# Decode steps around the attentions of a hybrid decoder: a pause, two closer paces, and key pages in quarters

## The chip, the cores and the metric

One Trainium2 chip, one of its cores. The metric is the device time of one execution of the whole program, in microseconds (us); of several runs the median is given. The engines are called by the names of the profile: PE (TensorE matmul) with its weight loads PEld, DVE (VectorE), ACT (ScalarE), POOL (GpSimd), SP (SyncE, which only issues DMAs here).

## What is computed

One inference step of a decoder layer for two groups that share the weights: a prompt of 1024 rows, and 8 sample rows that each look back on 8192 cached positions.

```
# prompt (1024 rows) and, with the same weights, samples (8 rows)
q, k, v, logf, u, z = mixer_inputs(rmsnorm(x), w_in)      # z: gelu, rmsnorm
x = x + concat(rmsnorm(fox_attend(q, k, v, logf)), rmsnorm(u * gate(z))) @ w_o
mk, mv = rmsnorm(mem) @ w_ck, rmsnorm(mem) @ w_cv         # prompt: 256 memory rows
x = x + cross_attend(rmsnorm(x), mk, mv) @ w_co           # samples: cached mk, mv
x = x + conv_ffn(rmsnorm(x))                              # 1024 -> 2 x 2816 -> 1024
```

The attention has 8 heads of 64 with a forget gate. For the samples its keys and values come from a paged cache (64 pages of 128 positions for each of 8 samples). The large products are done as three float32r matmuls of high and low parts.

## The kernel before, in words

**The prompt's work** is a chain of Python generators, and each `yield` states an estimate of the PE time that its piece takes. `p1` does the input projection: for q, the gates and u, k, v and z in turn, 8 tiles of 128 rows against 512 columns. The last four z tiles are done together (`by_rows(4, ws)`, L569): 8 yields of 2.6, then 4 of 0.1. Just ahead of them `early()` (L568) emits the first head pair's set-up of the first attention (L701 to L744) and the opening of `pmem`, which loads the memory rows and the first four blocks of `w_ck`. Then:

- `att0`: `attention(0)` for the first 512 rows (four head pairs, 8 score blocks each). `mix` sets beside it, yield for yield, a fill: `pmem`'s 8 products of 5.2 (2 weights x 2 column halves x 2 row tiles) and the first half of the gating (8 yields of 1).
- `att1`: `attention(1)` for the other 512 rows, without a fill.
- `mid0`, `ffn0`, `mid1`, `ffn1`: merge (transposes at L888), output projection, cross-attention and feed-forward for each half of the rows.

Weights come through `wload` (L249): SP issues a load of 512 KB into one of 4 `wr` buffers (L247), ACT writes the high part (L233), DVE the low part (L234), PE multiplies (L270 to L272). In the attention a score block (L759 to L763) is followed by its row maximum on DVE (L765, or L768 where it is two banks wide), the exponential on ACT (L766 or L769), transposes (L787) and the product with the values (L803). In `attention(1)` POOL copies half of the keys' high part (L735) and loads the gate rows (L709, L721).

**The samples' attention** is the generator `decode` (L1303 on), one step for each of 148 turns of its loop. A step gathers one K page of 128 x 2048 with an indirect DMA from POOL (L1354), multiplies it by the query on DVE (L1360) and reduces it to scores (L1364). Every second step gathers two V pages (L1413); the step after it multiplies them on PE (L1419). All K and V pages share four `kv` buffers. K's DVE work is queued behind the newest DVE instruction of the prompt (`behind(ENG.DVE)`), V's matmuls behind the newest of PE.

**Pacing.** The last loop of `build` sets the order: each yield `t` of the prompt is added to an account, and a decode step is emitted for every `PACE[phase]` in it, at most `int(t / PACE) + 1` of them for one yield. A step yields 1 itself; a smaller yield `w` puts back (1 - w) x PACE. `phase[0]` is the stage above, and `held` stops the decode in a few places. What runs after the cache is read (`sample_rest`) is paced by `rest`.

```
acc[0] += t
most = int(t / PACE[phase[1] or phase[0]]) + 1
while bgs and not held[0] and most and acc[0] >= PACE[phase[1] or phase[0]]:
```

The emitted order is not yet that of the engines: the framework's planner simulates the program, and each engine takes what is ready by order of emission. So a gather can start ahead of its place once a buffer is free.

`kstep` splits a page in two halves (`KS = 2`) in the attentions and the mid stages, and takes it whole elsewhere.

Of the kernel before, what the change touches and what calls it, by code (L numbers as in the profile page):

```python
# [12 lines left out]
ALU = mybir.AluOpType  # L13
AX = mybir.AxisListType
PSUM = bass.MemoryType.PSUM
ENG = mybir.EngineType
# [56 lines left out]
KS = 2  # L73
BKQ = 1
LA = (2, 2)
PACE = {'p1': 7.0, 'att0': 20.0, 'mid0': 8.0, 'ffn0': 8.5, 'att1': 15.0, 'mid1': 6.8, 'ffn1': 2.5, 'rest': 2.9}


def build(nc, tc, ctx, a, phases=None):
# [186 lines left out]
    def gemm3(out, pairs):  # L266

        n = len(pairs)
        for i, (sh, sl, mh, ml) in enumerate(pairs):
            mmul(out, sh, mh, start=(i == 0), stop=False)  # L270
            mmul(out, sh, ml, start=False, stop=False)  # L271
            mmul(out, sl, mh, start=False, stop=(i == n - 1))  # L272


    xsT = const.tile([P, 8, 32], F32, tag="xsT", name="xsT")
# [57 lines left out]
    def p1(early):  # L333
# [205 lines left out]
        for tt in range(8):  # L539
            if tt < 4:  # L540
                ps = BK()
                mm_chunk(tt, ws, ps, 0, 512)
                if tt == SD - 1:
                    sps = [sample_copy(*sps[0])]
                if tt == SD:
                    sp = sample_sum(*sps[0])
                    zs = T2()[:8]
                    nc.scalar.activation(zs, sp, AF.Gelu_apprx_tanh, scale=rsk)
                    ssv = sm([8, 1], "sss", 1)
                    ssq_into(ssv, zs)  # L550
                    r = rstd_of(ssv, AW, 1, "r1")
                    nc.vector.scalar_tensor_tensor(zs, zs, r, gs8, op0=ALU.mult, op1=ALU.mult)
                    nc.sync.dma_start(a["o_zs"], zs)

                    mxs = T2()[:8].rearrange("p (h d) -> p h d", d=64)
                    nc.vector.tensor_tensor(
                        mxs, zs.rearrange("p (h d) -> p h d", d=64), ws00[:, 0:8].unsqueeze(2).broadcast_to((8, 8, 64)), op=ALU.mult
                    )
                    nc.vector.tensor_tensor(mxs, mxs, ws00[:, 8:16].unsqueeze(2).broadcast_to((8, 8, 64)), op=ALU.add)
                    usv = us.rearrange("p (h d) -> p h d", d=64)  # L560
                    nc.vector.tensor_tensor(usv, usv, mxs, op=ALU.mult)
                    ssv = sm([8, 1], "sss", 1)
                    ssq_into(ssv, us)
                    r = rstd_of(ssv, AW, 1, "r1")
                    nc.vector.tensor_scalar(us, us, r, None, op0=ALU.mult)
                    nc.sync.dma_start(us_d, us)
            else:
                if tt == 4:  # L568
                    early()  # L569
                    pss = yield from by_rows(4, ws)  # L570
                ps = pss[tt - 4]
            z = T2()
            nc.scalar.activation(z, ps, AF.Gelu_apprx_tanh, scale=rstd[:, tt : tt + 1])
            ssq_into(ssz[:, tt : tt + 1], z)
            nc.scalar.dma_start(zg_d[tt * P : (tt + 1) * P, :], z)
            yield 5.2 if tt < 4 else 0.1
# [62 lines left out]
    def pmem():  # L639
        rm = const.tile([P, 2], F32, tag="rm", name="rm")  # L640
        ssm = sm([P, 2], "ssm", 1)
        for mt in range(2):
            t = U([P, D])
            nc.sync.dma_start(t, a["mem"][mt * P : (mt + 1) * P, :])
            ssq_into(ssm[:, mt : mt + 1], t)
        r = rstd_of(ssm, D, 2, "r2")
        nc.vector.tensor_copy(rm, r)
        mh, ml = [], []
        for q in range(2):
            h, l = U([P, 4, 256], F32R), U([P, 4, 256], F32R)  # L650
            raw = WRAW(1024).rearrange("p (k m) -> p k m", m=256)
            nc.sync.dma_start(raw, a["memT"][q * 512 : (q + 1) * 512, :].rearrange("(k p) m -> p k m", p=P))
            for k in range(4):
                kk = q * 4 + k
                split(raw[:, k, :], h[:, k, :], l[:, k, :], scale=gp[:, G_MEM + kk : G_MEM + kk + 1])
            mh.append(h)
            ml.append(l)
        ahead = [wraw(wpair(a["w_ck"], kk, 0, 512), 1024) for kk in range(4)]
        before = newest(ENG.Activation)
        yield 0.1  # L660
        for w, dst in ((a["w_ck"], mk_d), (a["w_cv"], mv_d)):
            for n in range(2):
                with tc.issue_after(before):
                    ws = [wload(wpair(w, kk, n * 512, 512), 1024, ahead.pop(0) if ahead else None) for kk in range(4)]
                for mt in range(2):
                    ps = MM()
                    ms_ = slice(mt * P, (mt + 1) * P)
                    gemm3(
                        ps[:, :512],
                        [  # L670
                            (mh[k // 4][:, k % 4, ms_], ml[k // 4][:, k % 4, ms_], ws[k // 2][0][:, k % 2, :], ws[k // 2][1][:, k % 2, :])
                            for k in range(8)
                        ],
                    )
                    t = T2()
                    nc.scalar.activation(t, ps[:, :512], AF.Copy, scale=rm[:, mt : mt + 1])
                    nc.scalar.dma_start(dst[mt * P : (mt + 1) * P, n * 512 : (n + 1) * 512], t)
                    yield 5.2


# [621 lines left out]
    def decode():  # L1302
# [48 lines left out]
        def kstep(b, ch, st):  # L1351
            qb, s = st
            kv = KV()
            nc.gpsimd.indirect_dma_start(kv, None, a["cache_k"], off(kidx[:, b, ch : ch + 1]))  # L1354
            kvv = kv.rearrange("p (k c) -> p k c", c=512)
            sp = KS if phase[0][:3] in ("att", "mid") or held[0] else 1
            m = 4 // sp
            with behind(ENG.DVE):
                for i in range(0, 4, m):
                    nc.vector.tensor_tensor(  # L1360
                        kvv[:, i : i + m, :], kvv[:, i : i + m, :], qb.unsqueeze(1).broadcast_to((P, m, 512)), op=ALU.mult
                    )
                for i in range(0, 4, m):
                    nc.vector.tensor_reduce(  # L1364
                        s[:, ch * 4 + i : ch * 4 + i + m, :].rearrange("p k h -> p (k h)"),
                        kvv[:, i : i + m, :].rearrange("p k (h d) -> p (k h) d", d=64),
                        axis=AX.X,
                        op=ALU.add,
                    )


        def soft_max(b, st, dt_):
# [31 lines left out]
        def soft_sum(b, lp):  # L1404
            ps = MS()
            with behind(ENG.PE):
                mmul(ps[:8, :1], lp, ones[:, 0:1], start=True, stop=True)
            nc.vector.tensor_copy(lT[:, b : b + 1], ps[:8, :1])
# [45 lines left out]
        for g in range(8 * 16 + 16 + VLAG + 2):  # L1454
            b, ch = divmod(g, 16)
            if ch == VLAG + 1 and 2 <= b < 10:
                vend(b - 2, vm[b - 2])
            if ch == 0 and 1 <= b < 9:
                dg[b - 1] = soft_all(b - 1, pm[b - 1])
            if ch == 1 and 1 <= b < 9:  # L1460
                lp[b - 1] = soft_exp(b - 1, st[b - 1], dg[b - 1])
            if ch == 2 and 1 <= b < 9:
                soft_sum(b - 1, lp[b - 1])
            if b < 8:
                kstep(b, ch, st[b])
                if ch == 11:
                    A[b] = gates_scan(b)
                if ch == 13:
                    dt_[b] = gates(b, A[b])
                if ch == 14 and b < 7:  # L1470
                    st[b + 1] = prep(b + 1)
                if ch == 15:
                    pm[b] = soft_max(b, st[b], dt_[b])
            if pend:

                pend.pop()()
                pend.pop()(newest(ENG.PE))
                if vch == 15:
                    vm[vb] = vmask(vb, dv[vb])
            vb, vch = divmod(g - 16 - VLAG, 16)  # L1480
            if 0 <= vb < 8 and vch % 2:
                if vch == 1:
                    dv[vb] = DV()
                pend += [vstep(vb, c, st[vb], dv[vb]) for c in (vch - 1, vch)]
            yield 1


    def rms8(src):
# [358 lines left out]
    for t in prompt():  # L1847
        ins = nc.cur_bb.bb.instructions
        for e in (ENG.DVE, ENG.PE):
            for i in range(len(ins) - 1, max(seen, len(ins) - 400) - 1, -1):  # L1850
                if ins[i].engine == e:
                    last[e] = ins[i]
                    break
        acc[0] += t
        most = int(t / PACE[phase[1] or phase[0]]) + 1
        while bgs and not held[0] and most and acc[0] >= PACE[phase[1] or phase[0]]:
# [100 lines left out]
```

## Time and profile before

| | us |
|---|---|
| median of 3 timed runs | 1864.72 |
| lowest and highest of them | 1860.55, 1866.24 |
| the profiled execution | 1858.95 |
| its span, first to last instruction | 1857.2 |
| PE busy | 1779.9 |
| DVE busy | 1390.5 |
| ACT busy | 749.2 |
| POOL busy | 488.5 |

All details below are of the profiled execution. A busy PE is not PE at its peak, since matmuls overlap and their ends are modelled; a PE that idles, or runs at a granted clock below 1, is time lost for certain. In rows of waits the engine ahead of the arrow stood idle, and what stands behind it released it. In a timeline the columns are the start, the length, engine, line, operation, output and inputs with their shapes, and the idle time before it in brackets.

### The profile page before, as it was taken

The numbers are of one execution on the slowest core, as the hardware profiler recorded it, in microseconds if no ns is written. First come the engines' busy times: TensorE is split into PE (matmuls) and PEld (weight loads), VectorE is DVE, ScalarE is ACT, GpSimd is POOL, SyncE is SP. The second block draws the span as 40 slices with busy tenths as digits, with TensorE's granted clock in tenths as the row PEclk, the third lists the DMA queues.
The fourth block names the chain that finished last, engine by engine and source line by source line (L and its number), as shares of the span: only waits on it lengthen the run. The fifth ranks groups of instructions, "written<-read, shape, count | busy, mean of one in ns | idle before, by whom it ended". The sixth has DMA issues, their size and how long they took to land.

```text
span 1857.2 us, 24238 instructions
## 1 busy us (share of the span) xinstructions
PE 1779.9 (96%) x9239; PEld 1290.3 (69%) x9239; DVE 1390.5 (75%) x1666; ACT 749.2 (40%) x1365; POOL 488.5 (26%) x437
## 2 busy tenths in 40 slices
PE   8999998878998999999999999999999999999998
PEld 5887666556676757777777777766576668767765
DVE  4788567876688787989989899898975549754344
ACT  6332355565633535332324234235353334232232
POOL 1243342242122222224332232233322111111110
PEclk9999999999999999999999999999999999999999
DMA  8877889684596976768768789988879588577971
GB/s 318 291 268 262 311 302 346 230 255 150 187 400 228 349 258 262 278 249 326 293 246 339 269 312 363 360 308 338 332 275 348 198 298 266 199 270 265 342 277 60
DMA packets 157012, 521.27 MB, mean 281 GB/s; under 512 B 20808, under 2 KB 40520, under 8 KB 124128
## 3 DMA queue, kind: packets, MB, share of 16 engines
q0 software_dynamic: 57168, 341.14, 49.0%
q1 hardware_dynamic: 92816, 165.99, 25.6%
q10 hardware_dynamic: 6912, 12.59, 1.8%
q8 instruction: 73, 1.20, 0.3%
q14 instruction: 43, 0.35, 0.1%
HBM read 495.73 MB, written 23.93 MB: 280 GB/s over the span
## 4 chain that ended last, share of the span: by engine, by line
PE 67%; DVE 10%; issue 9%; DMA 9%; ACT 4%; POOL 2%; SPq 0%; POOLq 0%; DVEq 0%; ACTq 0%
PE ba L270 9%; PE ba L271 9%; PE ba L272 9%; PE dv L1419 5%; PE bb L271 5%; PE bb L270 4%; PE bb L272 4%; DMA kv<-cache_v,kidx 2%; DVE kv L1360 2%; DMA kv<-cache_k,kidx 2%; DVE s L1364 2%; PE ba L1008 1%; DVE wl L234 1%; PE ba L1010 1%; PE ba L1009 1%
## 5 line engine op out<-in xcount | busy, mean ns | idle before, releaser
L233 ACT ACTIVATE wh<-wr 128x1024 fp32r<-128x1024 f32 (+2 forms) x220 | 229.0, 1044 | 493.1 <-PE ba L271 159.3
L234 DVE TENSOR_TENSOR wl<-wr,wh 128x1024 fp32r<-128x1024 f32 (+2 forms) x220 | 262.2, 1200 | 142.2 <-PE ba L272 54.5
L1354 POOL DMA_INDIRECT kv<-cache_k,kidx x128 | 185.3, 1448 | 611.5 <-DVE s L1364 376.6
L1360 DVE TENSOR_TENSOR kv<-kv,d 128x1024 f32<-128x1024 f32 (+1 forms) x185 | 295.6, 1628 | 42.6 <-DMA kv<-cache_k,kidx 42.5
L1364 DVE TENSOR_REDUCE s<-kv 128x16 f32<-128x1024 f32 (+1 forms) x185 | 295.9, 1619 | 0.1
L1413 POOL DMA_INDIRECT kv<-cache_v,kidx x128 | 171.3, 1338 | 294.4 <-PE dv L1419 191.9
L271 PE MATMUL ba<-u,wh 128*128 128x512 f32 (+1 forms) x560 | 220.6, 394 | 2.3 <-DVE u L237 2.1
L270 PE MATMUL ba<-u,wh 128*128 128x512 f32 (+1 forms) x560 | 219.8, 394 | 1.3 <-ACT u L236 1.1
L272 PE MATMUL ba<-u,wl 128*128 128x512 f32 (+1 forms) x560 | 219.7, 393 | 0.0
L270 PE MATMUL ba<-wh,u 128*128 128x512 f32 (+1 forms) x495 | 185.6, 378 | 1.4 <-DVE u L740 1.0
L271 PE MATMUL ba<-wl,u 128*128 128x512 f32 (+1 forms) x495 | 186.3, 377 | 0.0
L272 PE MATMUL ba<-wh,u 128*128 128x512 f32 (+1 forms) x495 | 184.2, 376 | 0.0
L1419 PE MATMUL dv<-kv,s 128*32 128x512 f32 x1024 | 130.5, 618 | 7.0 <-DMA kv<-cache_v,kidx 6.8
L270 PEld LDWEIGHTS ba<-u,wh 128*128 128x128 f32 x560 | 106.0, 190 | 33.8 <-issue 9.3
L271 PEld LDWEIGHTS ba<-u,wh 128*128 128x128 f32 x560 | 106.4, 190 | 33.1 <-issue 7.1
L272 PEld LDWEIGHTS ba<-u,wl 128*128 128x128 f32 x560 | 106.3, 190 | 32.5 <-issue 10.1
L271 PE MATMUL bb<-u,wh 128*128 128x512 f32 (+1 forms) x304 | 118.2, 389 | 1.7 <-DVE u L237 1.7
L270 PE MATMUL bb<-u,wh 128*128 128x512 f32 (+1 forms) x304 | 118.0, 389 | 0.5 <-ACT u L236 0.5
L272 PE MATMUL bb<-u,wl 128*128 128x512 f32 (+1 forms) x304 | 116.8, 384 | 0.0
L270 PEld LDWEIGHTS ba<-wh,u 128*128 128x128 f32 x495 | 92.9, 188 | 26.5 <-issue 5.9
L271 PEld LDWEIGHTS ba<-wl,u 128*128 128x128 f32 x495 | 93.1, 188 | 22.2 <-issue 5.9
L272 PEld LDWEIGHTS ba<-wh,u 128*128 128x128 f32 x495 | 93.1, 188 | 19.9 <-issue 3.1
(437 smaller groups left out, 3197.5 us busy)
## 6 DMA issues: line engine op xcount, KB each, us to landing
wr<-w_up SPq DMA_DIRECT2D x88, 512.0 KB
kv<-w_up POOLq DMA_DIRECT2D x22, 1024.0 KB, 7.0
wr<-w_down SPq DMA_DIRECT2D x40, 512.0 KB
kv<-w_down POOLq DMA_DIRECT2D x11, 1024.0 KB, 8.0
wr<-w_in SPq DMA_DIRECT2D x16, 512.0 KB
wr<-w_o SPq DMA_DIRECT2D x16, 512.0 KB
wr<-w_cq SPq DMA_DIRECT2D x16, 512.0 KB
wr<-w_co SPq DMA_DIRECT2D x16, 512.0 KB
```

What stands on the lines that cost most here:

```text
L233: nc.scalar.activation(h, src, AF.Copy)
L234: nc.vector.tensor_tensor(l, src, h.bitcast(F32), op=ALU.subtract)
L270: mmul(out, sh, mh, start=(i == 0), stop=False)
L271: mmul(out, sh, ml, start=False, stop=False)
L272: mmul(out, sl, mh, start=False, stop=(i == n - 1))
L1008: mmul(pss[i], mh[k][:, tb], wh, start=(k == korder[0]), stop=False)
L1009: mmul(pss[i], mh[k][:, tb], wl, start=False, stop=False)
L1354: nc.gpsimd.indirect_dma_start(kv, None, a["cache_k"], off(kidx[:, b, ch : ch + 1]))
L1360: nc.vector.tensor_tensor(kvv[:, i : i + m, :], kvv[:, i : i + m, :], qb.unsqueeze(1).broadcast_to((P, m, 512)), op=ALU.mult)
L1364: nc.vector.tensor_reduce(s[:, ch * 4 + i : ch * 4 + i + m, :].rearrange("p k h -> p (k h)"), kvv[:, i : i + m, :].rearrange("p k (h d) -> ...
L1413: nc.gpsimd.indirect_dma_start(kv, None, a["cache_v"], off(kidx[:, b, ch : ch + 1]))
L1419: mmul(dv[32 * j : 32 * j + 32, :], s[:, ch * 4 : ch * 4 + 4, :].rearrange("p k h -> p (k h)"), kvv[:, j, :], start=(ch == 1), stop=(ch == ...
```

## The change

Three edits in one, and nothing in what is computed.

- **Pause.** From the place where `early()` is called to the end of the first `pmem` product, yields of the prompt count 0 in the account, so that no decode step is emitted.
- **Paces.** A step for each 16 (before 20) in `att0`, and for each 10 (before 15) in `att1`.
- **Quarters.** In the attentions `kstep` becomes a sequence of four parts with a yield of 0.2 before each: multiply and reduce 512 columns of the page. The step then yields 0.2 more. In the mid stages the two halves stay, elsewhere the whole page.

```
-PACE = {'p1': 7.0, 'att0': 20.0, 'mid0': 8.0, 'ffn0': 8.5, 'att1': 15.0, 'mid1': 6.8, 'ffn1': 2.5, 'rest': 2.9}
+PACE = {'p1': 7.0, 'att0': 16.0, 'mid0': 8.0, 'ffn0': 8.5, 'att1': 10.0, 'mid1': 6.8, 'ffn1': 2.5, 'rest': 2.9}
...
+    paused = [False]
...
                 if tt == 4:
+                    paused[0] = True
                     early()
                     pss = yield from by_rows(4, ws)
...
                     nc.scalar.dma_start(dst[mt * P : (mt + 1) * P, n * 512 : (n + 1) * 512], t)
+                    paused[0] = False
                     yield 5.2
...
-            sp = KS if phase[0][:3] in ("att", "mid") or held[0] else 1
+            if phase[0][:3] == "att":
+
+                for i in range(4):
+                    yield 0.2
+                    with behind(ENG.DVE):
+                        nc.vector.tensor_tensor(kvv[:, i, :], kvv[:, i, :], qb, op=ALU.mult)
+                        nc.vector.tensor_reduce(
+                            s[:, ch * 4 + i, :], kvv[:, i, :].rearrange("p (h d) -> p h d", d=64), axis=AX.X, op=ALU.add
+                        )
+                return 0.2
+            sp = KS if phase[0][:3] == "mid" or held[0] else 1
...
+            return 1
...
+            left = 1
             if b < 8:
-                kstep(b, ch, st[b])
+                left = yield from kstep(b, ch, st[b])
...
-            yield 1
+            yield left
...
+        if paused[0]:
+            t = 0.0
         acc[0] += t
```

## The prediction

> **What bounds the kernel now.** I read the page first (busy shares, the 40 slices), then the busy table by stage, then the waits of PE and ACT in the stages that lose time, then the timelines there.
>
> ```profile
> PE 1779.9 (96%) x9239; PEld 1290.3 (69%) x9239; DVE 1390.5 (75%) x1666; ACT 749.2 (40%) x1365; POOL 488.5 (26%) x437
> PE   8999998878998999999999999999999999999998
> ```
>
> PE is busy for 1779.9 of 1857.2 us, so all that can be gained without removing matmuls is 77 us of idle time and whatever a lowered clock costs. Each digit is the busy share of 46.4 us in tenths: the weak slices are the first, the last, the seventh to tenth (279 to 464 us) and the thirteenth. Next the stages around the weak group.
>
> ```profile
> 224.00:263.00 39.00, 39.00 (x188) 29.03 (x187) 26.30 (x29) 21.21 (x41) 17.02 (x17) 1.00 0.81 284
> 263.00:295.00 32.00, 23.68 (x119) 14.55 (x118) 21.60 (x21) 15.03 (x32) 13.47 (x8) 0.89 1.03 400
> 295.00:340.00 45.00, 43.47 (x240) 32.78 (x239) 37.27 (x50) 29.50 (x60) 14.60 (x22) 1.00 0.82 290
> 263.00:385.00 122.00, 102.01 (x568) 71.53 (x567) 93.57 (x142) 68.77 (x160) 42.83 (x49) 0.94 0.85 308
> 385.00:512.00 127.00, 111.91 (x761) 78.71 (x761) 88.01 (x127) 81.45 (x173) 27.49 (x31) 0.95 0.59 184
> 512.00:560.00 48.00, 48.00 (x229) 36.01 (x228) 40.67 (x46) 18.61 (x32) 11.03 (x9) 1.00 1.02 399
> ```
>
> Columns: window, length, busy us of PE, PEld, DVE, ACT, POOL, granted clock, DMA share, GB/s. The last z tiles end at about 263; the first attention runs to about 385 with the memory's products between its pieces, the second to about 512. PE is full before (39.00 of 39.00) and after (48.00 of 48.00), and loses 20.0 us in the first attention and 15.1 in the second. The worst stretch is 263 to 295: 8.3 us idle and a clock of 0.89, with the DMA engines at a share of 1.03.
>
> ```profile
> 268.00:272.00 4.00, 0.65 (x5) 0.16 (x8) 2.22 (x5) 2.34 (x4) 1.31 (x1) 0.98 1.01 402
> 272.00:276.00 4.00, 4.00 (x20) 1.50 (x13) 0.31 (x1) 1.07 (x3) 1.80 (x2) 0.59 1.05 429
> 288.00:292.00 4.00, 2.51 (x14) 1.14 (x18) 3.42 (x4) 1.33 (x2) 0.00 (x0) 0.61 1.01 383
> ...
> PE dv L1419 <- DMA kv<-cache_v,kidx: 3.4, 1, 3.4
> PE ms L803 <- ACT t L794: 3.3, 2, 2.1
> PE ba L701 <- DMA t<-q_d: 1.0, 1, 1.0
> PE bb L787 <- ACT t L766: 0.7, 1, 0.7
> ...
> ACT wh L233 <- DMA wr<-w_ck: 6.6, 3, 2.9
> ACT wh L233 <- DMA wr<-w_cv: 2.8, 1, 2.8
> ```
>
> These four waits of PE (columns: us, times, longest) add up to 8.4 us, the whole idle time. Two name a DMA. The other two name ACT, and ACT itself had stood before its weight splits for 9.4 us of DMA: in the timeline below the split at 288.11 comes 1.01 us late, the copy L794 runs behind it at 289.07, and PE gets on at 289.49 after 2.06 us.
>
> ```profile
> 288.11 1.06 ACT L233 ACTIVATE wh<-wr 128x1024 fp32r<-128x1024 f32 x1 [1.01 <-DMA wr<-w_ck]
> 289.07 0.36 ACT L794 ACTIVATE t<-bb 128x256 f32<-128x256 f32 x1
> ...
> 289.49 1.54 PE L803 MATMUL ms<-t,u 128*64 128x256 f32 x6 [2.06 <-ACT t L794]
> ...
> 260.67 8.23 SPq L247 DMA_DIRECT2D wr<-w_ck  x4
> ...
> 263.14 2.88 POOL L1354 DMA_INDIRECT kv<-cache_k,kidx  x1 [0.19 <-issue]
> ...
> 282.20 1.73 POOL L1354 DMA_INDIRECT kv<-cache_k,kidx  x1 [2.67 <-DVE s L1364]
> ```
>
> Four weight loads of 512 KB are issued from 260.67 on; the last was split only at 288.11. From 263.14 to 282.20 five gathers of 1 MB each start (128 x 2048 x 4 bytes; the first and the last are shown), some 12.5 us of the DMA engines' time at the 402 to 429 GB/s of the rows. **So decode gathers starve the memory's weights here.** That stall is what the pause addresses.
>
> **The change, part by part.** First, how many decode steps move. I add up the yields. Behind the point where the pause begins stand 8 x 2.6 + 4 x 0.1 = 21.2 in p1; at a pace of 7 that is 3 steps, and the remainder carried into it makes it 4. The first attention yields 74.6, the fill (memory products, gating) 49.6: 124.2 / 20 = 6 steps. The second yields 74.6 / 15 = 5. Together 15. Afterwards: 0, then 124.2 / 16 = 7 and a part, then 74.6 / 10 = 7 and a part: again 15. From the first merge on, both kernels stand at the same step and have the same paces. So everything is decided between 245 and 512 us; what is gained there reaches the end, since PE is the bound behind it.
>
> *The pause.* A V pair and two K pages are gathered and then held through the pause, because their users are emitted behind it, and with four kv buffers no gather can start until the first is used. The next K step comes 16 units after the last count, some 14 us of yields after the first product: at about 280 on this clock. The five gathers above then do not stand beside the w_ck loads. The stretch 263 to 295 should look like 295 to 340, where the same products run with a loss of 1.53 in 45 us: 1.1 in 32. Idle time goes from 8.3 to 1.1: **-7.2 us**. The lowered clock cost (1 - 0.59) x 4.00 + (1 - 0.61) x 2.51 = 2.6 us beside it; I take **-2.5**. What is late next: on resuming, up to three gathers (3 MB, 7 us at 429 GB/s) start together near 285, when the w_cv loads are due. Bounds of this part: 0 (the stall only moves) and -11.
>
> ```profile
> 380.00:384.00 4.00, 2.45 (x11) 2.06 (x12) 3.34 (x6) 2.57 (x10) 2.35 (x4) 0.63 0.99 339
> 384.00:388.00 4.00, 4.00 (x17) 2.61 (x15) 2.35 (x8) 2.61 (x10) 0.00 (x0) 0.51 1.06 308
> ...
> 381.55 0.48 PE L787 MATMUL bb<-cp,t 128*128 128x128 f32 x1 [2.67 <-ACT t L766]
> ```
>
> The clock term rests on gaps of 3.35 us at most; here 2.67 us of idleness is followed by 0.63 and 0.51. [...]
>
> *Quarters.* Cost first.
>
> ```profile
> L1364 DVE TENSOR_REDUCE s<-kv 128x16 f32<-128x1024 f32 x22 | 26.3, 1207 | 0.1
> L1360 DVE TENSOR_TENSOR kv<-kv,d 128x1024 f32<-128x1024 f32 x22 | 25.8, 1215 | 0.0
> L1364 DVE TENSOR_REDUCE s<-kv 128x32 f32<-128x2048 f32 x3 | 6.8, 2279 | 0.0
> L1360 DVE TENSOR_TENSOR kv<-kv,d 128x2048 f32<-128x2048 f32 x2 | 4.6, 2288 | 4.2 <-DMA kv<-cache_k,kidx 4.2
> ```
>
> These are the K steps from 263 to 512: 63.5 us, 13 pages. Halving 2048 to 1024 saves 1.073 us, so 512 should take 1.215 - 0.536 = 0.68 us (multiply) and 0.67 (reduce). A page costs 2 x (1.215 + 1.207) = 4.84 us in halves and 4 x 1.35 = 5.40 in quarters. Fifteen pages in quarters are 81.0 us: **17.5 us more DVE work** in this stretch, nearly all of it in the second attention (6 pages become 8), whose DVE goes from 88 to about 102 of 127 us. [...]
>
> What they may save is the time for which a row maximum stands behind a K block:
>
> ```profile
> 363.56 2.33 DVE L1360 TENSOR_TENSOR kv<-kv,d 128x1024 f32<-128x1024 f32 x2
> 365.81 1.15 DVE L765 TENSOR_REDUCE mx<-ba 128x1 f32<-128x512 f32 x2
> 367.32 0.86 PE L787 MATMUL bb<-cp,t 128*128 128x128 f32 x3 [2.58 <-ACT t L766]
> ...
> 412.75 2.34 DVE L1360 TENSOR_TENSOR kv<-kv,d 128x1024 f32<-128x1024 f32 x2
> 415.13 1.23 DVE L768 TENSOR_REDUCE mx<-ba 128x1 f32<-128x1024 f32 x1
> 417.65 0.50 PE L759 MATMUL ba<-u,u 128*128 128x512 f32 x1 [2.59 <-ACT wr L769]
> ```
>
> Twice the scores are ready, DVE multiplies keys for 2.34 us, the maximum follows, then the exponential, and PE has stood for 2.6 us. A quarter's block is at most 1.35 us long, so each such stall shrinks by about 1 us; against that there are more blocks. All waits of PE for exponentials in both attentions are these two rows:
>
> ```profile
> PE bb L787 <- ACT t L766: 8.3, 6, 2.7
> PE ba L759 <- ACT wr L769: 5.9, 4, 2.6
> ```
>
> 14.2 us. Bounds: -7.1 (half goes) and +17.5 (all added DVE work reaches PE). DVE is idle for 39 us of the second attention, so I take the value near which both effects stand: **0**.
>
> *The V matmuls.*
>
> ```profile
> 224.00:263.00 39.00, 3.85 (x32) 0.83 (x32) 1.00 0.81 284
> 385.00:512.00 127.00, 5.77 (x48) 1.25 (x48) 0.95 0.59 184
> ```
>
> L1419 alone. One group of 16 (1.92 us) leaves the full stage for the second attention, which has 15.1 us of PE idle time: between 0 and -1.9. I take 0. Buffers and POOL: a K page keeps its buffer for four quarters, about 13 us (4 x 0.2 x 16), but two steps use four pages and take 249 / 15 x 2 = 33 us; nothing is charged. Each quarter is queued on DVE behind the newest main instruction, as the halves were; POOL's key casts and gate rows stand behind a gather that waits for a buffer, before and after.
>
> **The sum.** -7.2 - 2.5 + 0 + 0 = **-9.7 us**. The profiled execution took 1858.95 us (span 1857.2), 5.8 below the median of the timed runs; 1849.3 on its clock, and 1864.7 - 9.7 = **1855.0** as a median.
>
> **Rivals.**
> 1. *The starvation only moves.* The burst on resuming meets the w_cv loads, and PE waits near 290 to 310 as it did near 285. For it: the DMA share is still 0.82 at 290 GB/s in 295 to 340. Against: that stage lost only 1.5 us with gathers running. About -3: 1862.
> 2. *Quarters pay as well.* Half of the 14.2 us goes: -9.7 - 7.1, 1848. For it: the two stalls above. Against: 2.67 us at 381.55 has no K block near.
> 3. *DVE becomes the bound of the second attention* (slower). Place: row maximum and subtraction behind the queue of quarters at 80% load. Price 17.5, less 9.7: +7.8, 1872.5. It turns the gain into a loss from the point where 55% of the added DVE time reaches PE. For it: chain PE, DVE, ACT, PE with few score banks. Against: DVE is at 85% from 512 to 560 (40.67 of 48) and PE full, though without that chain.
> 4. *It does not do what it says.* The planner moves gathers up into the pause or the steps elsewhere, and the loads are as late as before: 1864.7. Against: buffers hold the gathers.
>
> **How the numbers follow.** Forecast (1851 to 1859) 0.48, rival 1 0.20, rival 2 0.14, rival 3 0.13, rival 4 0.05. The measurement of this kernel can tell about 0.3%, 5.6 us: faster is below 1859.1, slower above 1870.3. Faster: most of the forecast (0.43), rival 2 and a fifth of rival 1: 0.61. Slower: rival 3, 0.13. The rest, 0.26, is within. The range goes from rival 2's middle, 1847, to 1869: it leaves out about half of rival 2 and most of rival 3.
>
> **What would show it.** Right: no gather starts between about 250 and 280; from 263 to 295 PE idles under 3 us at a clock near 1; ACT's waits for w_ck are under 2 us; keys run as 128x512 at about 0.68 us; the first merge transposes come about 10 us earlier, and PE's losses in the second attention stay near 15 us. Wrong: waits for w_cv in place of those for w_ck (rival 1); PE's idle time in the second attention above 25 us, ended by ACT behind maxima (rival 3); gathers inside the pause (rival 4).

## The result, and the profile after

| | before | after |
|---|---|---|
| median of 22 timed runs each, us | 1864.92 | 1871.16 |
| lowest and highest | 1860.55, 1868.2 | 1864.22, 1883.45 |
| ratio, 95% interval | | 1.0034 [1.0023, 1.0046] |
| the profiled execution, us | 1858.95 | 1864.82 |
| its span | 1857.2 | 1862.9 |

The kernel became 6.2 us slower; 9.7 us faster was forecast. The two profiled executions stand 5.7 us of span apart, and each lies some 6 us below the median of its kernel, so they show about the same difference. First, the page of the changed kernel: busy times, and PE's and the clock's slices.

```profile
PE 1784.0 (96%) x9239; PEld 1290.3 (69%) x9239; DVE 1398.0 (75%) x1736; ACT 748.1 (40%) x1365; POOL 481.7 (26%) x437
PE   8999999878998999999999999999999999999998
PEclk9999999889999999999999999999999999999999
```

DVE has 70 instructions and 7.5 us more. The weak slices of PE are the same as before, but for the seventh (279 to 325 us), which is full now. The stages say more (columns as in the prediction).

```profile
224.00:263.00 39.00, 39.00 (x182) 30.43 (x181) 23.07 (x29) 22.30 (x44) 10.40 (x15) 1.00 0.88 305
263.00:295.00 32.00, 26.80 (x131) 19.70 (x130) 15.75 (x27) 20.11 (x43) 8.34 (x11) 0.89 0.62 196
295.00:340.00 45.00, 41.41 (x221) 31.02 (x221) 34.32 (x58) 25.17 (x53) 10.27 (x12) 0.96 0.80 287
263.00:385.00 122.00, 101.35 (x537) 72.62 (x535) 86.37 (x163) 66.07 (x152) 32.84 (x43) 0.89 0.75 251
385.00:512.00 127.00, 112.17 (x756) 73.79 (x757) 101.17 (x170) 79.49 (x175) 31.04 (x39) 0.97 0.65 215
512.00:560.00 48.00, 46.68 (x239) 33.83 (x238) 37.54 (x49) 19.06 (x33) 12.76 (x8) 1.00 0.94 367
```

From 263 to 295 the DMA share fell from 1.03 to 0.62, as meant, and the idle time from 8.3 to 5.2 us, but the clock is 0.89 as before. Over the whole first attention (263 to 385) nothing is left of that: 20.65 us idle (20.0 before) at a clock of 0.89 (0.94). In the second, 14.8 us idle (15.1 before).

Did the pause pause? The gathers on POOL, in the timeline of after:

```profile
241.02 0.94 POOL L1358 DMA_INDIRECT kv<-cache_k,kidx  x1 [1.19 <-DVE s L1378]
290.51 1.05 POOL L1428 DMA_INDIRECT kv<-cache_v,kidx  x1 [0.79 <-DVE s L1366]
```

No gather starts between 241.02 and 290.51. The products of `pmem` come out earlier for it. ACT's evacuations of the first, third, sixth and last product and the last exponential of the first attention, before:

```profile
278.14 0.69 ACT L676 ACTIVATE t<-ba,rm 128x512 f32<-128x512 f32 x1 [5.06 <-PE ba L272]
301.68 0.69 ACT L676 ACTIVATE t<-ba,rm 128x512 f32<-128x512 f32 x1 [1.30 <-PE ba L272]
328.12 0.68 ACT L676 ACTIVATE t<-ba,rm 128x512 f32<-128x512 f32 x1
348.31 0.69 ACT L676 ACTIVATE t<-bb,rm 128x512 f32<-128x512 f32 x1 [5.92 <-PE bb L272]
390.93 0.69 ACT L766 ACTIVATE t<-ba,mx 128x512 f32<-128x512 f32 x1
```

and after:

```profile
269.11 0.67 ACT L679 ACTIVATE t<-ba,rm 128x512 f32<-128x512 f32 x1
290.47 0.69 ACT L679 ACTIVATE t<-ba,rm 128x512 f32<-128x512 f32 x1 [3.00 <-PE ba L272]
319.11 0.69 ACT L679 ACTIVATE t<-ba,rm 128x512 f32<-128x512 f32 x1 [0.49 <-PE ba L272]
343.57 0.69 ACT L679 ACTIVATE t<-bb,rm 128x512 f32<-128x512 f32 x1 [0.34 <-PE bb L272]
389.87 0.69 ACT L770 ACTIVATE t<-ba,mx 128x512 f32<-128x512 f32 x1
```

Row by row the lead is 9.0, 11.2, 9.0, 4.7 and 1.1 us. It is only in part a stall removed. Up to the first product, all engines and then V's matmuls alone (L1419), before:

```profile
224.00:278.14 54.14, 50.79 (x246) 36.47 (x245) 35.97 (x39) 28.60 (x56) 25.56 (x22) 0.97 0.87 316
224.00:278.14 54.14, 7.20 (x48) 1.43 (x48) 0.97 0.87 316
```

and after (V's matmuls are L1434 here):

```profile
224.00:269.11 45.11, 45.11 (x213) 35.48 (x212) 23.92 (x31) 28.34 (x57) 10.40 (x15) 1.00 0.88 304
224.00:269.11 45.11, 1.92 (x16) 0.42 (x16) 1.00 0.88 304
```

PE idles 3.4 us less, and 5.3 us of V's matmuls are not done yet: most of the lead of 9.0 us is work put off. From 295 to the last exponential of the first attention the lead is spent again, before and then after:

```profile
295.00:390.93 95.93, 83.78 (x477) 59.80 (x476) 74.08 (x125) 57.26 (x139) 29.36 (x42) 0.95 0.80 273
```

```profile
295.00:389.87 94.87, 78.88 (x437) 55.45 (x437) 72.52 (x142) 50.21 (x125) 24.50 (x32) 0.89 0.76 257
```

PE idles 16.0 us there for 12.2, at a clock of 0.89 for 0.95. The first merge transposes, from the timeline of PE, before and then after:

```profile
503.20 1.47 PE L888 MATMUL ba<-cp,t 128*128 128x128 f32 x12
```

```profile
508.79 1.20 PE L892 MATMUL ba<-cp,t 128*128 128x128 f32 x9
```

The lead of 1.1 has become a lag of 5.6 us. From there to the end of the span both take the same time (1857.2 - 503.2 = 1354.0; 1862.9 - 508.8 = 1354.1). So the whole loss of the profiled execution arises ahead of the merge. The 6.7 us from lead to lag are lost in the second attention, here from its own start to the merge, before and then after:

```profile
390.93:503.20 112.27, 97.85 (x667) 69.18 (x667) 79.63 (x115) 72.55 (x156) 25.21 (x30) 0.95 0.54 166
```

```profile
389.87:508.79 118.92, 104.63 (x707) 68.60 (x706) 97.71 (x163) 72.93 (x156) 28.44 (x37) 0.97 0.67 222
```

PE is busy 6.8 us longer there and idles as long as before (14.3 us for 14.4). A part of that is new work. V's matmuls alone, in the windows 263 to 295 of before, and 263 to 295 and 385 to 512 of after:

```profile
263.00:295.00 32.00, 5.93 (x32) 1.11 (x32) 0.89 1.03 400
```

```profile
263.00:295.00 32.00, 1.92 (x16) 0.42 (x16) 0.89 0.62 196
385.00:512.00 127.00, 10.66 (x80) 2.21 (x80) 0.97 0.65 215
```

From 224 to 295 they fall from 64 to 32 (9.8 to 3.8 us with the window 224 to 263); in the second attention they rise from 48 to 80 (5.77 to 10.66 us). PE's idle time there did not shrink by these 4.9 us: in this kernel they came on top.

### The profile page after: what moved, and what is told of

The parts are those of the page before. It is cut to its first block, busy times and chain, and to the rows that moved or that the text cites. A ratio compares the mean times of both kernels' runs of the same rounds, so it can differ in the third digit from the quotient of the medians.

```text
span 1862.9 us, 24266 instructions
## 1 busy us (share of the span) xinstructions
PE 1784.0 (96%) x9239; PEld 1290.3 (69%) x9239; DVE 1398.0 (75%) x1736; ACT 748.1 (40%) x1365; POOL 481.7 (26%) x437
## 4 chain that ended last, share of the span: by engine, by line
PE 77%; DMA 9%; DVE 6%; issue 5%; ACT 3%; POOL 1%; SPq 0%; POOLq 0%; DVEq 0%; ACTq 0%
PE ba L270 11%; PE ba L272 11%; PE ba L271 11%; PE dv L1434 5%; PE bb L270 5%; PE bb L272 5%; PE bb L271 5%; DMA kv<-cache_k,kidx 2%; DMA kv<-cache_v,kidx 2%; PE ba L1012 1%; PE ba L1014 1%; PE ba L1013 1%; PE dv L1699 1%; PE bb L807 1%; DVE kv L1374 1%
## 5 line engine op out<-in xcount | busy, mean ns | idle before, releaser
L1358 POOL DMA_INDIRECT kv<-cache_k,kidx x128 | 171.2, 1337 | 598.8 <-DVE s L1378 342.0
L1374 DVE TENSOR_TENSOR kv<-kv,d 128x1024 f32<-128x1024 f32 (+1 forms) x156 | 258.2, 1682 | 30.5 <-DMA kv<-cache_k,kidx 30.1
L1378 DVE TENSOR_REDUCE s<-kv 128x16 f32<-128x1024 f32 (+1 forms) x156 | 258.5, 1674 | 0.0
L1428 POOL DMA_INDIRECT kv<-cache_v,kidx x128 | 179.0, 1399 | 299.2 <-PE dv L1434 241.8
L1434 PE MATMUL dv<-kv,s 128*32 128x512 f32 x1024 | 129.3, 603 | 2.8 <-ACT s L1414 1.9
```

Source lines behind the costliest of these rows:

```text
L1374: nc.vector.tensor_tensor(kvv[:, i : i + m, :], kvv[:, i : i + m, :], qb.unsqueeze(1).broadcast_to((P, m, 512)), op=ALU.mult)
L1378: nc.vector.tensor_reduce(s[:, ch * 4 + i : ch * 4 + i + m, :].rearrange("p k h -> p (k h)"), kvv[:, i : i + m, :].rearrange("p k (h d) -> ...
L1428: nc.gpsimd.indirect_dma_start(kv, None, a["cache_v"], off(kidx[:, b, ch : ch + 1]))
L1434: mmul(dv[32 * j : 32 * j + 32, :], s[:, ch * 4 : ch * 4 + 4, :].rearrange("p k h -> p (k h)"), kvv[:, j, :], start=(ch == 1), stop=(ch == ...
```

## Experiments

Three edits, each there or not, make eight kernels: the kernel before, the changed one and six between them. What an experiment does not name is as in the kernel before. "First merge" is the start of the first merge transposes in the profiled execution, "rest" the time from there to the end of its span. "Steps" counts the whole decode steps emitted by the first merge, from the yields. Each profiled execution is a single one, and some stand well off the median of their kernel: before, after and e9, for instance, 6.0, 6.3 and 8.5 us below it, e1, e10 and e6 7.5, 5.1 and 5.5 us above. So differences of a few us in "first merge" and "rest" are uncertain.

**One edit alone, and two together.** Theories: the denser decode costs; the quarters cost; what the pause gains is lost on the way whatever stands beside it.

e1, the pause alone (paces and halves as before):

```
+                    paused[0] = True
                     early()
...
+                    paused[0] = False
                     yield 5.2
...
+        if paused[0]:
+            t = 0.0
```

> The pause alone, old paces and halves; 4 decode steps fewer before the first merge. Load theory (the closer paces bring DVE and PE work into the attentions, and that costs what the pause gains): the gain of about 9 us stands, 1856. Quarter theory (the cutting costs): also 1856. Lost-anyway theory (the first attention's tail without the fill is bound by its own chain, so products that end earlier only wait there): 1862 to 1866, first merge at 500 to 504.

e2, the paces alone:

```
-'att0': 20.0, ... 'att1': 15.0
+'att0': 16.0, ... 'att1': 10.0
```

> The closer paces alone (16 and 10), halves, no pause; 4 decode steps more before the first merge. Load theory: slower than before by 6 to 15 us, 1871 to 1880. Quarter theory: no change, 1865. Lost-anyway theory: says nothing of this one beyond a DMA stall at least as long as before near 263 to 295.

e3, the quarters alone:

```
+            if phase[0][:3] == "att":
+                for i in range(4):
+                    yield 0.2
...
+                return 0.2
```

> Quarters alone, old paces, no pause; the same steps before the first merge as before. Load theory: 13 pages by 0.55 us more, 0 to +7 us, 1865 to 1872, most likely 1866. Quarter theory: +10 to +15, 1875 to 1880.

e4, the pause of e1 with the paces of e2, in halves:

> The change without the quarters. Load theory: as the whole change, 1871, or some us above it, since the blocks of 2.3 us stay. Quarter theory: the gain of the pause comes through, 1856. Lost-anyway theory: 1865 to 1871.

e5, the pause of e1 with the quarters of e3:

> Pause and quarters with the old paces. Theory that quarters cost wherever they are (8 to 13 us in the pairs measured so far): 1875 to 1880, 10 above the pause alone. Theory that the quarters hurt only where much decode work falls into the attentions: 1867, as the pause alone.

e6, the paces of e2 with the quarters of e3:

> The closer paces with quarters, without the pause. Sum of parts: paces alone and quarters alone each gave about 13 us over the kernel before, so together about 1890. Placement (the kernel before stands at a favourable order that any shift of the steps loses, once): about 1877, 1873 to 1881, like each of the two alone. Under placement the pause, which is all that the changed kernel has more than this one, is worth 5 to 10 us; under sum of parts it is worth about 19.

| | edits | median us | ratio to before, 95% | steps | first merge | rest |
|---|---|---|---|---|---|---|
| before | none | 1864.9 | | 41 | 503.2 | 1354.0 |
| e1 | pause | 1867.2 | 1.0013 [1.0001, 1.0026] | 37 | 502.5 | 1370.3 |
| e2 | paces | 1877.7 | 1.0073 [1.0052, 1.0093] | 45 | 514.9 | 1357.9 |
| e3 | quarters | 1877.8 | 1.0065 [1.0041, 1.0089] | 40 | 510.1 | 1368.0 |
| e4 | pause, paces | 1861.1 | 0.9985 [0.9971, 0.9999] | 41 | 505.7 | 1355.5 |
| e5 | pause, quarters | 1869.7 | 1.0028 [1.0013, 1.0043] | 36 | 496.6 | 1372.5 |
| e6 | paces, quarters | 1874.5 | 1.0056 [1.0039, 1.0072] | 45 | 518.4 | 1359.8 |
| after | all three | 1871.2 | 1.0034 [1.0023, 1.0046] | 41 | 508.8 | 1354.1 |

Every edit stands in four pairs of kernels that differ by it alone. At the first merge the pause gives -0.7, -9.2, -13.6 and -9.6, **-8.3 us** on the mean; the paces +11.7, +3.2, +8.3 and +12.2, **+8.9**; the quarters +6.9, -5.9, +3.6 and +3.1, +1.9. The pause takes four steps out of the time ahead of the merge, and the closer paces put four or five back. On the mean that is some 2 us for a step, but the single pairs scatter as widely as the means are large.

The pair that is the forecast's own, e1 against the kernel before, gives only -0.7 us, with four steps less to do and nothing put back. Its first product comes out 8.8 us earlier (269.34), its last exponential of the first attention 3.3 us earlier (387.61). All engines of e1:

```profile
263.00:295.00 32.00, 28.72 (x142) 20.94 (x141) 16.38 (x23) 22.41 (x47) 10.03 (x11) 0.95 0.75 274
295.00:387.61 92.61, 76.01 (x429) 55.00 (x427) 64.64 (x111) 49.65 (x123) 23.77 (x32) 0.93 0.70 230
```

From 263 to 295 PE idles 3.3 us for 8.3, and from there to the last exponential 16.6 us for 12.2. Most of the idle time that the pause removes comes back behind it, with the old paces and halves. Of the 16.6 us, 4.2 are waits for DMAs: the gate rows, which POOL issues behind the gathers, and keys:

```profile
PE ba L765 <- DMA u<-ck_d: 2.8, 1, 2.8
PE ba L733 <- DMA t<-o_k: 1.4, 1, 1.4
```

Nor do the closer paces cost in one place. In e2 the first attention ends 12.1 us later than in before (403.07), and the second takes 0.5 us less, though V's matmuls rise there from 48 to 64: PE's idle time in it falls from 14.4 to 12.0 us. In after, against e5, the first attention ends 0.1 us earlier, and the second takes 12.4 us longer.

Behind the merge the steps count again. Rows with 36 or 37 steps take 14.8 to 18.4 us more there than their like with 41 (e1 against before and e4, e5 against after), of which several us can be the choice of the profiled execution; the rows with 45 have no further gain, and e3, with 40, takes 1368.0 for a reason that is not known. Where it is lost shows in one window, PE alone of these columns, e1 and then e4:

```profile
1500.00:1700.00 200.00, 190.83 (x881) 134.23 (x880) 133.82 (x192) 71.61 (x115) 29.45 (x45) 0.98 0.69 238
```

```profile
1500.00:1700.00 200.00, 198.48 (x968) 144.18 (x967) 133.21 (x191) 68.99 (x110) 30.02 (x46) 1.00 0.73 252
```

With four steps behind, PE idles 9.2 us there at a clock of 0.98, for 1.5 us at 1.00. In this window all four kernels with 36 to 38 steps (e1, e5, and e10 and e18 below) idle 7.2 to 9.2 us, and all others 0.9 to 3.1. That the sample rows' work then comes late beside the prompt's last stages is the likely reason, and not shown. So the pause by itself leaves a price at the end.

The medians add up less well: the pause gives +2.3, -16.6, -8.1 and -3.3 in the four pairs, the paces +12.8, -6.0, -3.3 and +1.5, the quarters +12.9, +2.5, -3.2 and +10.0. No sign is settled by one pair. On the mean over the whole program it is the quarters that cost 5.6 us and the paces 1.2: the other way round than at the merge.

Of the theories, e1 speaks for the one that the gain is lost on the way (its merge lies in the 500 to 504 of that theory, its median just above 1866), e2 for the denser decode, e3 for the quarters. e4 is in the range of none, e5 between its two. e6 is in the range of placement, 15 us below the sum of the parts.

**Is it the size or the spreading of the key parts?** e7 is the whole change with all four quarters emitted in one place; e8 the whole change with two halves, each behind a yield of 0.4.

```
                 for i in range(4):
-                    yield 0.2
                     with behind(ENG.DVE):
...
-                return 0.2
+                return 1
```

> The whole change, but the four quarters of a page are emitted in one place, without a yield between them. Spread theory (a page cut over four places keeps its buffer longer and puts key work ahead of every attention step): as the pause with the paces and halves, 1861. Small-instruction theory (twice the DVE instructions and 0.55 us a page): 15 pages by 0.55 are 8 us, as the whole change, 1869 to 1871.

```
-                for i in range(4):
-                    yield 0.2
+                for i in range(0, 4, 2):
+                    yield 0.4
```

> The whole change, but a page in two halves with a yield of 0.4 ahead of each. Spread theory: as the whole change, 1871. Small-instruction theory: as the pause with the paces, 1861.

e7: 1871.8 us, 1.0040 [1.0025, 1.0054]. e8: 1875.9 us, 1.0062 [1.0043, 1.0082]. Both are as slow as the change. e7 differs from e4 in little but the size of the parts, e8 in little but their spreading, and either costs over 10 us (1861.1 for e4). So neither theory has it alone.

**Does any shift lose?** e9 and e17 shift the paces by one, without the pause; e10 and e18 are the same with the pause of e1. All have halves.

```
-'att0': 20.0, ... 'att1': 15.0
+'att0': 19.0, ... 'att1': 14.0
```

> The kernel before with paces of 19 and 14 for 20 and 15: one decode step more before the first merge, the places of the others shifted. Any theory of load: 1865 to 1867. If the order of the engines alone decides (where a step falls between the attention's loads and its maxima), it can be off by 5 to 13 us, as the paces of 16 and 10 (12.8) and the quarters alone (13) were.

> The pause on top of the neutral shift (paces 19 and 14, halves), whose own time was 1876.4. Placement: the pause is worth its forecast against a shifted kernel, 6 to 10 us: 1866 to 1870. Pause is worthless by itself: 1874 to 1879. Pause harms: above 1880.

```
-'att0': 20.0, ... 'att1': 15.0
+'att0': 21.0, ... 'att1': 16.0
```

> The kernel before with slightly wider paces (21 and 16 for 20 and 15), two halves, no pause: fewer steps in the attentions. Chance (the kernel before is a favourable order, any shift loses): 1869 to 1880, the last exponential of the first attention at 396 to 406, for 390.9 before. Density (a closer decode is what loses): at or under the kernel before, 1860 to 1866.

> The same with the pause. If the pause is worth what was forecast of it, against the same order without it: 5 to 12 us under the run with 21 and 16 alone, and the first attention ends 8 to 12 us earlier than there. If its mean so far was made by the shifts: no faster than without it.

| | paces | pause | median us | ratio to before, 95% | steps | first merge | rest |
|---|---|---|---|---|---|---|---|
| e9 | 19, 14 | no | 1876.4 | 1.0067 [1.0042, 1.0091] | 42 | 506.6 | 1359.5 |
| e10 | 19, 14 | yes | 1868.2 | 1.0018 [1.0005, 1.0032] | 38 | 499.7 | 1371.8 |
| e17 | 21, 16 | no | 1872.0 | 1.0041 [1.0019, 1.0062] | 40 | 511.1 | 1353.8 |
| e18 | 21, 16 | yes | 1875.1 | 1.0059 [1.0039, 1.0079] | 36 | 499.9 | 1373.6 |

One step more or fewer at the merge costs 12 or 7 us in the median, although all three kernels stand at step 62, from the yields, when the merge stage is over: the kernel before is a favourable order, and its neighbours on both sides are worse. Against its own neighbour the pause brings the merge forward again, by 6.8 and 11.1 us, and again the rest takes 12 and 20 us longer with 38 and 36 steps (e9 and e17 were profiled 8.5 and 5.2 us below their medians, e10 5.1 above, so these two sizes are rough). The last exponential of the first attention and the first merge, from the timelines of e9 and of e10:

```profile
398.02 0.69 ACT L769 ACTIVATE t<-ba,mx 128x512 f32<-128x512 f32 x1
506.55 1.47 PE L891 MATMUL ba<-cp,t 128*128 128x128 f32 x12
```

```profile
380.57 0.69 ACT L770 ACTIVATE t<-ba,mx 128x512 f32<-128x512 f32 x1
499.72 1.47 PE L892 MATMUL ba<-cp,t 128*128 128x128 f32 x12
```

17.5 us ahead there, 6.8 at the merge. The median of e10 is in the range expected of a pause that pays against a shifted kernel; e18 is not (3.1 us slower than e17, where 5 to 12 less was expected), although its first attention ended 8.5 us earlier, as expected. All six pairs with and without the pause together: the merge -8.5 us on the mean (-0.7 to -13.6), the median -5.1 us (+3.1 to -16.6).

**Is it given back by the loads?** On SP the loads of the queries wait for a row buffer (t2). SP's longest wait ahead of them from 280 to 400, in before, e10 and after:

```profile
SPq L688 <- DMA o_mk<-t: 4.9, 1, 4.9
```

```profile
SPq L692 <- PE ms L807: 27.0, 2, 17.8
```

```profile
SPq L692 <- PE ms L807: 28.1, 2, 19.7
```

A wait of 5 us has become one of 20. But the load behind it, the first queries of the second attention, starts only 1.3 us later than in before: SP had come to it earlier. Before and after:

```profile
363.98 0.36 SPq L688 DMA_DIRECT2D t<-q_d  x1
```

```profile
365.27 0.36 SPq L692 DMA_DIRECT2D t<-q_d  x1
```

e12 is the whole change with one row buffer more, for which the decode gives one; e13, e15 and e16 are the kernel before, e4 and e9 with the same two lines; e14 is the change with the decode's buffer taken and none given. e11 is the change with the fill at two thirds of its rate, so that it lasts as long as the first attention.

```
-NT = 7
+NT = 8
...
-tag="d2", bufs=5
+tag="d2", bufs=4
```

> The whole change with one more row buffer (8 t2 for 7), paid for by one buffer less of the decode's d2 (4 for 5). Load theory: SP's longest wait ahead of the queries' load falls from 20 us to under 10, PE's wait for that load (2.5 us) and the waits behind it go, the first merge comes 4 us or more earlier (at or before 505) and the median is 1864 to 1867. Rival (that wait is off the path): the first merge stays within 3 us of 508.8 and the median is 1868 to 1875; a decode short of d2 could add to it.

> The kernel before with 8 t2 and 4 d2. Give-back theory (the wait for a row buffer is what the denser, earlier decode brings): SP's longest waits ahead of the queries' load are only 5 us here, so the buffer gains at most 3 us: 1861 to 1866. Rival (the buffer speeds up any of these kernels): 1849 to 1856, and the change then is no faster than this kernel with the same buffers.

> The whole change with 4 d2 and still 7 t2. If the row buffer does it: 1869 to 1877, as the change. If the decode's lacking buffer does it (it holds steps back): 1853 to 1860.

> Pause and paces with halves, 8 t2 and 4 d2. If the quarters cost by their DVE work (17.5 us at most, 8 by halves of it): 1843 to 1850, 6 to 12 under the run with quarters. If their cost was one of order that the buffer takes away: 1853 to 1860, the same as with quarters.

> The neutral shift (19 and 14, halves, no pause) with 8 t2 and 4 d2; without them 1876.4. If what a shift loses is the wait for row buffers: 1862 to 1868, back at the kernel before. If the loss of a shift is elsewhere: 1872 to 1878.

```
-MIXR = 1.0
+MIXR = 0.67
```

> The whole change, with the fill (memory products, gating) mixed into the first attention at two thirds of the rate, so that it lasts to the end of it. Fill theory (what the pause gains is given back because the first attention's last blocks run without other matmuls): PE's idle time from 340 to 390 falls from about 12 us to under 6, the last exponential of the first attention comes 4 to 6 us earlier, and the median is 1863 to 1867. Rival (loads queued in order on SP, or the second attention): the idle time only moves to the place where the memory's products were denser, and the median is 1868 to 1878.

| | kernel | t2, d2 | median us | ratio to before, 95% | first merge | rest |
|---|---|---|---|---|---|---|
| e12 | after | 8, 4 | 1855.8 | 0.9957 [0.9941, 0.9974] | 503.8 | 1349.2 |
| e14 | after | 7, 4 | 1862.3 | 0.9991 [0.9973, 1.0009] | 504.6 | 1349.4 |
| e13 | before | 8, 4 | 1867.3 | 1.0021 [1.0007, 1.0035] | 508.9 | 1355.4 |
| e15 | e4 | 8, 4 | 1870.4 | 1.0024 [1.0005, 1.0042] | 508.4 | 1360.1 |
| e16 | e9 | 8, 4 | 1879.2 | 1.0074 [1.0053, 1.0095] | 521.1 | 1359.6 |
| e11 | after, fill at 0.67 | 7, 5 | 1866.4 | 1.0013 [1.0003, 1.0023] | 512.8 | 1357.5 |

e12 by itself would look like proof: the whole change, and 1855.8 us, where 1855.0 was forecast. Its controls take it away. The buffer makes e4 9 us slower (e15), does nothing for e9 (e16), and 8.9 of e12's 15.4 us are there without it (e14). e14 and e15 are in none of the ranges that the theories gave them, and e16 lies just above the one for a loss elsewhere. In e12 the wait is still 13.8 us long:

```profile
SPq L692 <- PE bb L791: 25.6, 4, 13.8
```

and e10 reaches the end of its first attention 10.4 us ahead of the kernel before with a wait of 17.8 us. So the load theory falls as the cause, and so does "a buffer speeds up any of these kernels" (e13, 1867.3, is over both theories' figures). e11's median is what the fill theory wanted, but its profile says the reverse: the first attention ends at 396.5, 6.6 us later than in after, and PE stands 8.4 us for the gating's weights:

```profile
PE ba L609 <- DVE u L601: 8.4, 1, 8.4
```

Its gain is not explained by that theory. e12 and e14 also have the 80 V matmuls of after in the second attention (10.66 us), and yet their first merge comes at 503.8 and 504.6: these matmuls alone do not make the loss either. e12 is nevertheless the best kernel of all, below the kernel before by 0.43%; what makes this order good is not known.

## Why the prediction was wrong

- **The step that failed: "what is gained there reaches the end, since PE is the bound behind it", with -7.2 and -2.5 for the pause.** The stall at the w_ck loads did go: no gather starts from 241 to 290, and nothing waits for w_ck from 263 to 295. But PE still idles 5.2 us there and not under 3, at a clock of 0.89 as before: what became late next were the copy L798 and the queries, in PE's waits:

```profile
PE ms L807 <- ACT t L798: 2.8, 1, 2.8
PE ba L705 <- DMA t<-q_d: 2.4, 1, 2.4
```

  So where the pause acts the two terms measured -3.1 and 0, and even this was not kept: from 295 to the last exponential PE idles 3.8 us longer at a lower clock, and both attentions together idle 35.5 us for 35.1. PE was not the bound behind it. By the prediction's own rows 10.1 of the 20.0 us of idle time in the first attention lie from 340 to 385. e1, which has this term alone, reaches the merge 0.7 us earlier, for 9.7. Which chain brings the idle time back in after stays open: PE's waits from 295 to the last exponential name ACT and DVE alone there, while e1 also has 4.2 us of DMAs.
- **The size of the lead was luck.** In all six pairs the first product comes out 8.1 to 9.4 us earlier, near the 9.7. But in after 5.3 us of its lead are V matmuls put off, which the two terms do not contain. Against the kernels other than before the pause brings the merge 6.8 to 13.6 us forward, with four steps less done: its worth depends on the order that it meets.
- **What is put off comes back: "between 0 and -1.9. I take 0", for the V matmuls.** Two groups went to the second attention, not one (48 to 80 matmuls), and their 4.9 us stand beside an idle time that stayed (14.4, now 14.3). Since 5.9 us of them had left 224 to 295, 0 is near the balance of the move; but then their leaving is no part of a gain. The prediction puts the closer paces themselves at no cost: over four pairs they cost 8.9 us at the merge, and 1.2 in the medians.
- **"From the first merge on, both kernels stand at the same step": right, and it mattered.** Both take 1354 us from there; with 36 to 38 steps it is 1370 to 1374 (and 1368 in e3, with 40).
- **Quarters, 0 of -7.1 to +17.5.** The duration was right: 0.68 us was worked out for 512 columns, and the groups of after from 263 to 512 show 680 and 677 ns.

```profile
L1365 DVE TENSOR_TENSOR kv<-kv,d 128x512 f32<-128x512 f32 x60 | 40.2, 680 | 0.0
L1366 DVE TENSOR_REDUCE s<-kv 128x8 f32<-128x512 f32 x60 | 39.8, 677 | 0.4
```

  The effect on the merge, +1.9 on the mean of four pairs from -5.9 to +6.9, is near the 0 taken; in the medians it is +5.6, from -3.2 to +12.9. Both means lie within the bounds, and neither is settled.
- **The rivals.** Starvation that moves: not to the w_cv loads, for which ACT waits 1.3 us; that the idle time moves is right, in after without a DMA in PE's waits behind 295, in e1 with 4.2 us of them. DVE as the bound of the second attention: the sign is that of the result and DVE does 101.17 of 127 us there, but the idle time did not rise above 25 us as that rival needed; it is 14.8, and e4, without quarters, also has its merge later than before. Work that is only put off was not among them.
- **The range left out the order itself.** Shifts by one step (e9, e17) cost 12 and 7 us. By the four-pair means the change would come to -8.3 + 8.9 + 1.9 = +2.5 us at the merge, and it has +5.6; the remainder is of the size of that scatter. Four orders without the pause and with 40 to 42 steps (before, e3, e9, e17) have 1864.9, 1877.8, 1876.4 and 1872.0: the start was the best of them by 7 us. So an average gain of 5 us from a pause does not show against it.

Shown: the stall at the w_ck loads goes with the pause; in this kernel its gain is not kept, with or without the other two edits (after, e1); more than half of the lead at the first product is work put off; the kernels with 36 to 38 steps have 7.2 to 9.2 us of PE idle time from 1500 to 1700, all others 0.9 to 3.1. Not settled: which chain brings the idle time back, where the steps put back cost, and what makes one order 7 to 12 us better than its neighbour. Neither SP's wait, nor V's matmuls, nor the size or the spreading of the key parts, nor the fill's length decides it alone.

## What to carry to other kernels

When a stall is removed, look whether the engine is the bound in the stage right behind. Here it was not, and 5.0 us of idle time removed became 4.4 us more of it further on (e1). Keep apart what is removed and what is only put off: at the first product 5.3 of 9.0 us were put off. Price work that is moved as on the path where it lands, even if the engine has idle time there: in the changed kernel 4.9 us of matmuls beside 14 us of idleness shortened none of it, while in e2 one group shortened it by 2.4 us. In a kernel whose order is made by a planner, run one or two neutral shifts (a pace by one) before believing any single kernel's 5 us, and test a good one by its controls.

## What the runs showed of the hardware

**The spread of the runs goes with the clock.** The 22 runs of after go from 1864.22 us (mean granted clock 0.988) to 1883.45 (0.976), with a standard deviation of 4.9 us; time by granted clock goes from 1835.9 to 1842.6, with one of 1.9. In the clock records of after's trace, every stretch at a clock of 0.50 lasts 3.413 us or two or three times that, but for the last one, which runs past the end of the span. The first of them in the attention starts at 279.10, around two waits of PE with 1.0 us of matmuls between them (277.68 to 278.70); the timeline of PE, and the windows ahead of the fall and behind it (PE's time and the clock, third from the right):

```profile
277.68 0.65 PE L807 MATMUL ms<-t,u 128*64 128x256 f32 x2 [2.75 <-ACT t L798]
281.14 1.12 PE L705 MATMUL ba<-cp,t 128*128 128x128 f32 x4 [2.45 <-DMA t<-q_d]
```

```profile
275.69:279.10 3.41, 1.01 (x4) 0.39 (x4) 3.10 (x7) 2.32 (x6) 0.00 (x0) 1.00 0.86 277
279.10:285.93 6.83, 4.79 (x17) 4.00 (x18) 1.94 (x3) 3.59 (x9) 0.01 (x1) 0.50 0.47 168
```

So here gaps of 2.75 and 2.45 us went with a loss. A stretch of 3.413 us at 0.50 costs at most 1.7 us of PE's time (half of its length; an estimate from these records). In the 3.41 us ahead of the fall PE was busy for 1.0 us, its longest idle stretch in them was 2.0 us, and the second wait had only begun.
